# A DeltaNet, gating and Fourier step: the last base inverse is stepped beside the scan, inverse buffers get a pool of their own, inverses are stored in two halves

## The chip, the cores and the metric

The kernel runs on one core of a Trainium2 chip. The metric is the device time of one execution in microseconds; less is better. The core has TensorE for matrix products (PE, with its weight loads as PEld), VectorE (DVE), ScalarE (ACT), GpSimd (POOL), and SyncE (SP), which here only issues DMAs. Each engine works through its own list of instructions in order.

## The reference, cut to what matters

One layer of a model with three parallel token mixers, for 2048 sample tokens and 128 context tokens, width 1024:

```python
qkv, beta, dec, z_a, u_b, v_b, z_b, x_c, z_c, gates = jnp.split(xn @ w_in, points, -1)
o_a = rmsnorm(delta_bidir(l2norm(q), l2norm(k), v, g, beta, s0_f, s0_b)) * silu(z_a)
o_b = chunk_sgu(u_b, v_b, ...) * silu(z_b)
o_c = fourier_mix(x_c, grid) * silu(z_c)
pb = jnp.einsum('btnw,nwd->btnd', jnp.stack([o_a, o_b, o_c], 2), w_branch)
out = jnp.einsum('btnd,btnd->btd', sigmoid(gates), pb) @ w_out
# delta_bidir, per chunk and direction:
m = eye + b * (k k^T) * dec_strict            # unit lower triangular
u = solve(m, b * v - b * exp(gam) * k S)      # the reference solves for both parts first
o = exp(gam) * q S + ((q k^T) * dec_incl) u
S = exp(gam_last) * S + kd^T u                # S goes from chunk to chunk
```

The triangular solve and the walk of the state S over the chunks, forward and backward, are what the change is about.

## The kernel before, in words

Products are taken in pairs of 16-bit numbers (high and low part, three matmuls for one product; the helper with line L161 issues all of them). The sequence of the program is: normed x and z_a; q, k, v with their convolution; then the main line of big matrix products, which is the gating branch (to about 700 us), the Fourier branch (line numbers around L1243 to L1340, to about 1047 us), a first merge (the gating branch), a second (Fourier, to about 1720 us), a third (delta) and the output product.

The delta branch has no place of its own in this line. It is a generator, `delta()`, that a pace steps. After each unit of the main line the pace gets a number of units (`pace.tick`, `pace.part`), and it takes one step of the generator for each `quota` units: 1.6 during the preparation, 1.3 (`SCAN`) from the scan on. The order in which the program is written so mixes both; a scheduler that honours a few priorities then sets each engine's list from it. The same pace also moves the conversion of the weights along (`weight_step`).

The delta branch has these parts. 17 tiles of 128 tokens (tile 16 is the context) are prepared in five groups: (16), (0 to 3), (4 to 7), (8 to 11), (12 to 15). `prep` writes for each tile k, q, v, the products and the 32x32 diagonal blocks of the triangular matrices (nd) to DRAM. `base_inverse(g)` then inverts all diagonal blocks of a group at once on VectorE: 31 rounds of a product (L795, the tile names are XB and E) and a subtraction (L796), then a split into 16-bit halves on ACT and VectorE, and two stores (L805) to the DRAM array ei. The inverse of a group is stepped together with the preparation of the next group. The last group's has no next preparation: `for _ in base_inverse(4): yield 1` steps it alone, in 841 to 884 us. Then the memory pool of preparation and inverses (dqa) is closed, and one for the scan (dqb) is opened in its place.

`scan()` walks 34 iterations: forward over tiles 16, 0, 1, ... 15, then backward over 16, 15, ... 0. It has three chains. `level` builds the 128x128 inverses R from the 32x32 ones, reading ei (tiles ES, Q, T, R, N; cleared once in `zeroed`, L813, by POOL; evictions at L860 to L896). The chain of the state scales k (skn, L970), makes `v = sv - k S` (L908 after L907: the split into 16 bits, for v, u and S alike), `sv = R v` (L1001), u and the new S. `attend` makes the outputs o. The first S of a direction is scaled at L1024. A finished tile goes out through `finish`.

The Fourier branch evicts its products with copies and mirrored copies on VectorE (tiles X2, printed as X; L1285 to L1287), yT (L1304, L1305), and gates them on POOL (st, L1137), which stores them (br, L1139). At the merges' start the memory of the Fourier constants (cfp) is given back and the branch weights' pool (bwp) opened; `converting` makes from a staged weight (wst) its square sum with the scratch in blo (L209), the scaled high part (bhi, L222) and the low part (L223). Memory is shared in this way all over: a tile in a later pool waits for whatever lay at its address in the closed one.

Of the kernel before, what the change touches and what calls it, by code (L numbers as in the profile page):

```python
# [14 lines left out]
AF = mybir.ActivationFunctionType  # L15
ALU = mybir.AluOpType
# [4 lines left out]
P = 128  # L21
# [8 lines left out]
EPS = 1e-6  # L30
C_QKV, C_BD, C_ZA, C_U, C_V, C_ZB, C_XC, C_ZC, C_G = 0, 1536, 1552, 2064, 2576, 3088, 3600, 4112, 4624
QUOTA = 1.6
SCAN = 1.3
MT = 0.015
XB = 4
AD = (0, 2, 4, 6)
CQ = 545
FS = 4096.0
# [73 lines left out]
def hybrid_flow_kernel(ctx: ExitStack, tc: tile.TileContext, x_prompt, x_sample, state_delta, c, c_ctx, ln_g, w_ada,  # L112
# [3 lines left out]
    V, A, G, PE, SY = nc.vector, nc.scalar, nc.gpsimd, nc.tensor, nc.sync  # L116
    uid, rot = [0], [0]

    def nm(s):
        uid[0] += 1  # L120
        return f"{s}_{uid[0]}"

    def pool(stack, name, bufs, **kw):
        return stack.enter_context(tc.tile_pool(name=name, bufs=bufs, **kw))

    def sb(pl, shape, tag, dt=F32, bufs=None):
        kw = {} if bufs is None else {"bufs": bufs}
        return pl.tile(list(shape), dt, tag=tag, name=nm(tag), **kw)
# [17 lines left out]
    def dram(name, shape, dt=F32):  # L146
        return drp.tile(list(shape), dt, tag=name, name=name)
# [30 lines left out]
    def scales(ss, pl, tag, sb16=None):  # L178

        ps = bank(ps_x, [P, 1])  # L180
        mm(ps, ones16, widened(ss, pl, tag) if sb16 is None else sb16)
        t = sb(pl, [P, 4], tag)
        V.tensor_copy(t[:, 0:1], ps)
        h = t[:, 3:4].bitcast(I32)
        V.tensor_scalar(h, t[:, 0:1].bitcast(I32), 24, None, ALU.logical_shift_right)
        V.tensor_scalar(t[:, 1:2].bitcast(I32), h, -8388608.0, 204.0 * 8388608, ALU.mult, ALU.add)
        V.tensor_scalar(t[:, 2:3].bitcast(I32), h, 8388608.0, 50.0 * 8388608, ALU.mult, ALU.add)
        return t[:, 1:2], t[:, 2:3]
# [253 lines left out]
    for ti, (t0, tn) in enumerate(TBS):  # L442
        if t0 not in xts:
            load_x(t0, tn)
        g = 0 if t0 < NS else 1
# [10 lines left out]
        for k in range(KT):  # L456
# [3 lines left out]
            t = sb(p0p, [P, tn], "xm", bufs=3)  # L460
# [17 lines left out]
    def h3(ap):  # L478
        return ap.rearrange("p (h x) -> p h x", h=H)
# [7 lines left out]
    vqs = sb(dp, [P, 12], "vqs")  # L487
    decD = [dram(f"dec{t}", [P, 2, WB]) for t in range(NCH)]
    qkvD = dram("qkv", [12, P, LP - 2])
    dl = ExitStack()  # L490
    dq = pool(dl, "dqa", 1, side="right")
    cfs = ExitStack()
    CN = _CW - _CF
    cf = sb(pool(cfs, "cfp", 1), [P, 2, CN], "cf", F16)
# [16 lines left out]
    def decays():  # L511
# [71 lines left out]
        def rows_of(t):  # L583
            if t % 5 in (0, 1):
                row = sb(dq, [P, 2, WB], "dc", bufs=2)
            elif t % 5 == 2:
                row = sb(dq, [P, 1024], "E").rearrange("p (d x) -> p d x", d=2)
            else:
                if t % 5 == 3:
                    xb[0] = sb(dq, [P, 2048], "XB")  # L590
                row = xb[0][:, (t % 5 - 3) * 1024:(t % 5 - 2) * 1024].rearrange("p (d x) -> p d x", d=2)
            row = row.rearrange("p d (h i) -> p d h i", h=H)
            for d in range(2):
                SY.dma_start(row[:, d], gamR[d, t * H:(t + 1) * H, :].rearrange("h (o i) -> o h i", o=1).to_broadcast([P, H, P]))
            return row
# [5 lines left out]
        xb = [None]  # L601
# [20 lines left out]
    for ct in range(12):  # L622
        w = getw(1, 2 if ct < 6 else min(4, 15 - ct))
        for half in range(1):
# [12 lines left out]
            y = sb(a1p, [P, LP - 2], "cy")  # L637
# [26 lines left out]
    eD = [dram(f"ei{g}", [2, 32, len(ts), H * 512], F16) for g, ts in enumerate(GROUPS)]  # L664
# [109 lines left out]
    def base_inverse(g):  # L774
        nt = len(GROUPS[g])
        nb = 16 * nt
        XB = sb(dq, [P, 2048], "XB")
        X, tmp = XB[:, 0:1024], XB[:, 1024:2048]
        E = sb(dq, [P, 1024], "E")
        if nt < 4:  # L780
            V.memset(X, 0.0)
            V.memset(tmp, 0.0)
        b3 = lambda t_: t_.rearrange("p (j i) -> p j i", j=32)
        for d in range(2):
            SY.dma_start((X if d == 0 else tmp)[64 * d:64 * d + nb, :], ndD[g][d].rearrange("t h (b j) i -> (t h b) (j i)", b=4))
        for _ in range(8):
            yield 0
        V.tensor_copy(b3(X[64:P, :]), tmp[64:P, :].rearrange("p (i j) -> p j i", j=32))
        G.memset(E, 0.0)
        G.memset(E[:, 0:1024:33], 1.0)  # L790
        X3, E3 = b3(X), b3(E)
        for k in range(31, 0, -1):
            n_ = 32 - k
            t3 = tmp[:, 0:k * n_].rearrange("p (j i) -> p j i", j=k)
            V.tensor_tensor(t3, X3[:, 0:k, k:k + 1].to_broadcast([P, k, n_]), E3[:, k:k + 1, k:32].to_broadcast([P, k, n_]), ALU.mult)  # L795
            V.tensor_tensor(E3[:, 0:k, k:32], E3[:, 0:k, k:32], t3, ALU.subtract)  # L796
            if k % 2 == 0:
                yield 1
        both = XB.bitcast(F16).rearrange("p (j l w c) -> p j l w c", j=32, l=2, w=2)
        for w, src in ((0, E3), (1, E.rearrange("p (i j) -> p j i", j=32))):  # L800
            A.activation(both[:, :, 0, w, :], src, AF.Copy, scale=FS)
            V.scalar_tensor_tensor(both[:, :, 1, w, :], src, FS, both[:, :, 0, w, :], ALU.mult, ALU.subtract)
            yield 1
        for d in range(2):
            SY.dma_start(eD[g][d].rearrange("j t (y x) -> (t y) j x", x=128),  # L805
                         both[64 * d:64 * d + nb].rearrange("p j l w c -> p j (l w c)"))
            yield 1

    odd, wide, q_st, q_hi = [1], [], [], []

# [250 lines left out]
    def bounds():  # L1061

        nonlocal qs, us
        s0 = sb(dq, [P, 2, WB], "tok")
        for d in range(2):
            SY.dma_start(h3(s0[:, d]), state_delta[0, 0, d].rearrange("h k v -> k h v"))
        yield 1
        A.activation(sb(dq, [P, 1024], "E"), s0.rearrange("p d x -> p (d x)"), AF.Square, scale=math.sqrt(8.0), accum_out=vqs[:, 4:5])
# [14 lines left out]
    def delta():  # L1083
        nonlocal dq
        seq = [(g, ci, t) for g, ts in enumerate(GROUPS) for ci, t in enumerate(ts)]
        held = {1: rows(1, 16), 2: rows(2, 16), 0: rows(0, 16), "dc": decay_rows(16)}
        yield from bounds()
        base = iter(())
        for i_, (g, ci, t) in enumerate(seq):
            if ci == 0 and g:  # L1090
                for r_ in base:
                    if r_:
                        yield 1
                base = base_inverse(g - 1)
            for n_, _ in enumerate(prep(g, ci, t, seq[i_ + 1][2] if i_ < 16 else None, held)):
                yield 1
                if next(base, 0):
                    yield 1
        late(None, None)
        for r_ in base:  # L1100
            if r_:
                yield 1
        for _ in base_inverse(4):
            yield 1
        dl.close()
        dq = pool(dl, "dqb", 1, side="right")
        V.tensor_scalar(rq, rq, bnds[:, 2:3], None, ALU.mult)
        V.tensor_scalar(beta, beta, FS, None, ALU.mult)
        for d in range(2):
            V.tensor_tensor(eg[:, d], eg[:, d], rq, ALU.mult)  # L1110
        pace.quota, pace.fine = SCAN, True
        yield from scan()
        dl.close()
        dps.close()

    pace.start(delta(), QUOTA)


# [115 lines left out]
    for g in range(4):  # L1234
        xw, zw = getw(2, 2)
        for gh in range(1):
# [23 lines left out]
            for q in range(0, NCH, 4):  # L1260
                qn = min(4, NCH - q)
                ps = bank(ps_mm, [P, qn, P])
                for i in range(qn):
                    t = q + i
# [65 lines left out]
                gate_unit(2, g, ti, zw, yT[:, t0:t0 + tn], fronts[ti] if ti < 3 else silu_unit(ti, zw, zc), ti > 2)  # L1330
    fs.close()
    cfs.close()


    mD = dram("mrg", [KT, P, NTOK])
# [226 lines left out]
```

## Time and profile before

| what | value |
|---|---|
| median of 3 runs | 2200.02 us (2197.28 to 2202.29) |
| the profiled execution | 2200.34 us, its span 2198.2 us, mean granted clock 0.993 |
| scan | about 885 to 1686 us |
| last base inverse | about 841 to 884 us |

Times in the excerpts are microseconds from the start of the span unless marked ns. In a list of groups (`line engine op out<-in ... xN | busy, mean ns | idle before, releaser`) the number behind the second bar is the idle time of the engine just before these instructions, followed by what ended most of it. In a list of waits the three numbers are the sum, the number of waits and the longest. In the timeline a row has the start, the length, the engine, the line, operation and tile, and in brackets how long the engine stood still before it and what ended that. A table by stretches has the stretch, its length, then the busy time of PE, PEld, DVE, ACT, POOL (instructions in brackets), the mean granted clock of TensorE (1.00 is full speed), the busy share of the DMA engines, and GB/s.

### The profile page before, as it was taken

How to read it: one execution, taken by the hardware profiler on the slowest of the kernel's cores; microseconds unless marked ns; L12 is line 12 of the kernel's file. 1: busy time of each engine (PE TensorE's matmuls, PEld its weight loads, DVE VectorE, ACT ScalarE, POOL GpSimd, SP SyncE). 2: the span in 40 equal slices, each digit the busy share in tenths (PEclk: the TensorE clock that was granted, in tenths of full speed). 3: DMA queues.
4: the chain of work that ended last, by engine and by line, in shares of the span. 5: the costliest groups of instructions: out<-in, count | busy, mean ns of one | idle time of the engine just before them, and what ended most of it. 6: DMA issues, size and time to landing. Idle time of an engine off the chain costs nothing. (4 is left out here: it accounts for less than half of the span.)

```text
span 2198.2 us, 42667 instructions
## 1 busy us (share of the span) xinstructions
PE 2125.9 (97%) x16234; PEld 1213.1 (55%) x16234; DVE 1311.2 (60%) x3140; ACT 1014.4 (46%) x2345; POOL 707.5 (32%) x862
## 2 busy tenths in 40 slices
PE   7999999999999999899899999999999999999998
PEld 3565444455555587777555555555654444444443
DVE  5746745469979698466665555765674544223454
ACT  3644644345466474355544445655553422222332
POOL 1421433223333322432322223344532221222543
PEclk9999999999999999999999999999999999999999
DMA  8324733167777662444655556776664544324542
GB/s 280 141 87 149 260 117 110 61 203 231 241 229 239 198 192 83 126 130 137 203 172 162 164 164 185 240 212 209 200 198 151 168 125 133 118 78 123 174 148 103
DMA packets 304568, 365.09 MB, mean 166 GB/s; under 512 B 39426, under 2 KB 215787, under 8 KB 302315
## 3 DMA queue, kind: packets, MB, share of 16 engines
q1 hardware_dynamic: 289226, 302.19, 45.6%
q0 software_dynamic: 12688, 51.27, 6.4%
q10 hardware_dynamic: 2448, 8.91, 1.0%
q8 instruction: 127, 2.08, 0.4%
q14 instruction: 79, 0.64, 0.1%
HBM read 234.67 MB, written 127.62 MB: 165 GB/s over the span
## 5 line engine op out<-in xcount | busy, mean ns | idle before, releaser
L161 PE MATMUL b<-xh,whi 128*128 128x512 f16 (+1 forms) x1920 | 652.8, 349 | 0.4 <-DVE mrow L1391 0.4
L161 PE MATMUL b<-xl,whi 128*128 128x512 f16 (+1 forms) x1920 | 652.9, 348 | 0.0
L161 PE MATMUL b<-xh,wlo 128*128 128x512 f16 (+1 forms) x1920 | 651.9, 348 | 0.5 <-DVE wlo L223 0.5
L161 PEld LDWEIGHTS <-whi 128*128 128x128 f16 x3904 | 358.8, 98 | 330.0 <-issue 9.4
L161 PEld LDWEIGHTS <-wlo 128*128 128x128 f16 x1952 | 191.7, 98 | 180.8 <-issue 5.0
L161 PE MATMUL b<-big,bhi 128*128 128x512 f16 (+1 forms) x960 | 250.6, 347 | 2.4 <-ACT big L1355 1.9
L1395 POOL TENSOR_TENSOR mrow<-mrow,sg 128x512 f32<-128x512 f32 (+1 forms) x80 | 91.8, 1148 | 293.9 <-DVE sg L1394 225.7
L161 PE MATMUL b<-big,blo 128*128 128x512 f16 (+1 forms) x480 | 162.9, 347 | 0.0
L1385 ACT ACTIVATE sg<-b,winv 128x512 f32<-128x512 f32 (+1 forms) x120 | 74.1, 618 | 174.5 <-PE b L161 173.7
L644 POOL TENSOR_TENSOR cy<-cy,raw 128x545 f32<-128x545 f32 (+1 forms) x48 | 74.9, 1586 | 184.2 <-ACT raw L643 184.2
L161 PEld LDWEIGHTS <-xh 128*128 128x128 f16 x1496 | 117.0, 98 | 28.1
L1394 DVE SCALAR_TENSOR_TENSOR sg<-b,binv,sg 128x512 f32<-128x512 f32 (+1 forms) x80 | 53.4, 667 | 126.1 <-PE b L161 119.3
L161 PEld LDWEIGHTS <-bhi 128*128 128x128 f16 x960 | 86.5, 98 | 73.6 <-issue 2.1
L175 DVE CAST wscb<-wss 128x1 bf16<-128x1 f32 x93 | 14.3, 154 | 148.5 <-ACT wlo L209 67.3
L864 POOL COPY T<-ES 32x256 f16<-32x256 f16 x68 | 30.5, 449 | 202.3 <-DMA ES<-ei 167.1
L161 PE MATMUL b<-whi,xh 128*128 128x128 f16 x544 | 92.9, 219 | 0.0
L161 PE MATMUL b<-wlo,xh 128*128 128x128 f16 x544 | 92.9, 219 | 0.0
L161 PE MATMUL b<-whi,xl 128*128 128x128 f16 x544 | 92.9, 219 | 0.0
L161 PE MATMUL b<-wohi,mh 128*128 128x512 f16 x240 | 90.9, 379 | 1.4 <-ACT mh L1462 1.4
L161 PE MATMUL b<-wohi,ml 128*128 128x512 f16 x240 | 90.8, 379 | 0.3 <-DVE mscb L175 0.3
L161 PE MATMUL b<-wolo,mh 128*128 128x512 f16 x240 | 90.9, 379 | 0.0
L209 ACT ACTIVATE wlo<-wst 128x1024 f16<-128x1024 f32 x52 | 55.0, 1057 | 77.5 <-DMA wst<-in_w_in_dram 74.1
(456 smaller groups left out, 4285.4 us busy)
## 6 DMA issues: line engine op xcount, KB each, us to landing
wst<-in_w_in_dram SPq DMA_DIRECT2D x60, 512.0 KB, 4.9
qkv<-cy POOLq DMA_DIRECT2D x12, 1089.0 KB, 5.4
st<-br SPq DMA_DIRECT2D x48, 256.0 KB, 4.6
mrow<-mrg SPq DMA_DIRECT2D x18, 512.0 KB, 3.6
mrow<-mrg SPq DMA_DIRECT2D x16, 576.0 KB
mrg<-mrow POOLq DMA_DIRECT2D x16, 576.0 KB, 3.6
dc<-dec SPq DMA_DIRECT2D x17, 512.0 KB, 4.7
kq<-qkv SPq DMA_DIRECT2D x34, 256.0 KB, 4.6
```

The lines of the kernel that those rows point to most:

```text
L161: PE.matmul(out, l, r, start=start, stop=stop)
L175: V.tensor_copy(sb16, ss)
L209: A.activation(w.lo, st, AF.Square, accum_out=ss)
L644: G.tensor_tensor(y[:, c0:c1], y[:, c0:c1], raw[:, 1 + c0:1 + c1], ALU.mult)
L864: G.tensor_copy(T16[rows(a0, b), :, :, b], ES[0:32, :, 2 * a0 + b, :, wT])
L1385: A.activation(sg, ps, AF.Sigmoid, scale=gw.inv)
L1394: V.scalar_tensor_tensor(sg, ps, binv[:, 1:2], sg, ALU.mult, ALU.mult)
L1395: G.tensor_tensor(mr, mr, sg, ALU.add)
```

## The change

Three edits. First, E and XB, the buffers of the inverse (also used as scratch by two earlier steps), move from the pool dqa to one of their own, dqx, of 12288 bytes per partition, on the other side of the memory, open until the Fourier branch ends. Second, `base_inverse(4)` is no longer run to its end before the scan: the pool dqa is closed at once, and one step of the inverse is taken after each step of the scan; SCAN goes from 1.3 to 1.39. Third, each inverse is split and stored in two halves of 16 columns.

```diff
-SCAN = 1.3
+SCAN = 1.39
...
     dq = pool(dl, "dqa", 1, side="right")
+    dxs = ExitStack()
+    dx = pool(dxs, "dqx", 1)
...
-        XB = sb(dq, [P, 2048], "XB")
+        XB = sb(dx, [P, 2048], "XB")
         X, tmp = XB[:, 0:1024], XB[:, 1024:2048]
-        E = sb(dq, [P, 1024], "E")
+        E = sb(dx, [P, 1024], "E")
...
-        for w, src in ((0, E3), (1, E.rearrange("p (i j) -> p j i", j=32))):
-            A.activation(both[:, :, 0, w, :], src, AF.Copy, scale=FS)
-            V.scalar_tensor_tensor(both[:, :, 1, w, :], src, FS, both[:, :, 0, w, :], ALU.mult, ALU.subtract)
-            yield 1
-        for d in range(2):
-            SY.dma_start(eD[g][d].rearrange("j t (y x) -> (t y) j x", x=128),
-                         both[64 * d:64 * d + nb].rearrange("p j l w c -> p j (l w c)"))
-            yield 1
+        for js in (slice(0, 16), slice(16, 32)):
+            for w, src in ((0, E3), (1, E.rearrange("p (i j) -> p j i", j=32))):
+                A.activation(both[:, js, 0, w, :], src[:, js], AF.Copy, scale=FS)
+                V.scalar_tensor_tensor(both[:, js, 1, w, :], src[:, js], FS, both[:, js, 0, w, :], ALU.mult, ALU.subtract)
+                yield 1
+            for d in range(2):
+                SY.dma_start(eD[g][d, js].rearrange("j t (y x) -> (t y) j x", x=128),
+                             both[64 * d:64 * d + nb, js].rearrange("p j l w c -> p j (l w c)"))
...
-        for _ in base_inverse(4):
-            yield 1
+        base = base_inverse(4)
         dl.close()
         dq = pool(dl, "dqb", 1, side="right")
...
-        yield from scan()
+        for _ in scan():
+            yield 1
+            next(base, 0)
...
     fs.close()
     cfs.close()
+    dxs.close()
```

**In units of the pace** (counted in both programs; main-line units at which the delta branch reaches a place):

| place | before | after |
|---|---|---|
| last base inverse begins | 584.1 | 584.1 |
| scan begins (iteration 0) | 625.6 (655.1) | 584.1 (614.1) |
| iteration 17 (backward direction) | 920.2 | 897.8 |
| scan ends | 1189.0 | 1185.1 |
| first merge begins | 741.6, in iteration 5 | 741.6, in iteration 7 |
| second merge begins | 1002.7, in iteration 22 | 1002.7, in iteration 23 |
| last block of the second merge | 1231.2 | 1231.2 |

So an iteration takes (1189.0 - 655.1)/34 = 15.7 units before and (1185.1 - 614.1)/34 = 16.8 after.

**In memory.** Before, the scan's tiles S16, sk, o and sq_ lie on the places of XB and E. After, the first tiles of the scan (skn, sv, R, T, Q, N) lie on places of tiles loaded for the preparation (kq, qr), and S, kn16, v16 and sqk on those of n32 and n16. The Fourier constants lie 12288 bytes higher, and the weights' pool of the merges, which lay on their place before, now lies on the place of E.

**In the order of the engines.** First POOL, around the last gates of a Fourier group (st, stored as br) and the clearing of the scan's buffers (MEMSET). Before:

```order
L1139 DMA br_4087<-st_9463 128x512
L1137 TENSOR_TENSOR st_9497<-sg_9494,yT_8310 128x512
L1137 TENSOR_TENSOR st_9564<-sg_9561,yT_8310 128x128
L1139 DMA br_4087<-st_9497 128x512
L1139 DMA br_4087<-st_9564 128x128
L813 MEMSET R_1320_10487 128x1024
L813 MEMSET T_1321_10489 128x512
```

Now:

```order
L758 DMA nd_4098<-nd_9462 128x4x32 x2
L1140 TENSOR_TENSOR st_9476<-sg_9068,yT_8331 128x512
L1140 TENSOR_TENSOR st_9480<-sg_9138,yT_8331 128x512
L1140 TENSOR_TENSOR st_9484<-sg_9253,yT_8331 128x512
L815 MEMSET R_1272_9724 128x1024
L815 MEMSET T_1273_9726 128x512
```

The clearing stood behind a whole group's gates and stores, and now stands behind the first three gates of that group, right after the preparation's last store.

Second VectorE, around the scan's first row v (L908, now L910). Before:

```order
L1286 COPY X_1140_8304<-X_1140_8304 128x8x63
L1285 TENSOR_TENSOR X_1140_8304<-b_10337,X_1140_8304 128x4x63
L1304 TENSOR_TENSOR yT_9569<-b_10356,us_10381 128x8x32
L1305 TENSOR_TENSOR yT_9569<-b_10356,us_10381 128x8x32
L1287 TENSOR_SCALAR X_1140_8304<-X_1140_8304 128x8x63
L908 SCALAR_TENSOR_TENSOR v_1362_11064<-sv_10485,v_1362_11064 128x512
L1285 TENSOR_TENSOR X_1141_8305<-b_10395,X_1141_8305 128x4x65
L1286 COPY X_1141_8305<-X_1141_8305 128x8x63
L1024 TENSOR_SCALAR S_11058<-S_11058,usc_4243 128x512
```

Now:

```order
L797 TENSOR_TENSOR XB_9747<-XB_9747,E_9748 128x135
L798 TENSOR_TENSOR E_9748<-E_9748,XB_9747 128x27x5
L797 TENSOR_TENSOR XB_9747<-XB_9747,E_9748 128x156
L798 TENSOR_TENSOR E_9748<-E_9748,XB_9747 128x26x6
L910 SCALAR_TENSOR_TENSOR v_1323_10422<-sv_9722,v_1323_10422 128x512
L797 TENSOR_TENSOR XB_9747<-XB_9747,E_9748 128x175
L798 TENSOR_TENSOR E_9748<-E_9748,XB_9747 128x25x7
L1273 SCALAR_TENSOR_TENSOR xc_9695<-b_9598,xc_9695 128x512
L797 TENSOR_TENSOR XB_9747<-XB_9747,E_9748 128x192
L1026 TENSOR_SCALAR S_10416<-S_10416,usc_4246 128x512
```

Row v stood between two copies X of the Fourier branch; now it and the scaling of S stand among the rounds of the inverse (L797, L798), with a Fourier eviction (xc, L1273) between them.

Third ACT at the start of the first merge, between the first high part of a branch weight (bhi, L222) and the square sum of the second (blo, L209). Before:

```order
L222 ACTIVATE bhi_13405<-wst_11422,wsc_13413 128x512
L907 ACTIVATE u_13325<-sv_13071 128x512
L1385 ACTIVATE sg_13526<-b_13458,winv_12235 128x512
L894 ACTIVATE Q_10497<-b_13559 64x256
L860 ACTIVATE Q_1322_10491<-b_13626 32x256
L972 CAST kn_1600_13536<-skn_13499 128x512
L862 ACTIVATE Q_1322_10491<-b_13626 32x256
L209 ACTIVATE blo_14053,wss_14054<-wst_13741 128x512
L879 ACTIVATE R_1320_10487<-b_13650 64x4x64
L907 ACTIVATE S_1593_13482<-S_11058 128x512
```

Now:

```order
L222 ACTIVATE bhi_13821<-wst_11872,wsc_13829 128x512
L1141 ACTIVATE sg_13428,oss_481_4093<-st_13662 128x512
L909 ACTIVATE u_13714<-sv_13409 128x512
L209 ACTIVATE blo_14449,wss_14450<-wst_14137 128x512
L1389 ACTIVATE sg_13961<-b_13874,winv_12687 128x512
L896 ACTIVATE Q_9734<-b_13946 64x256
```

Six rows stood between bhi and blo, and two stand there now.

More of the change, by code (lines that the diff above doesn't have):

```diff
@@ L586, in rows_of @@
             elif t % 5 == 2:
-                row = sb(dq, [P, 1024], "E").rearrange("p (d x) -> p d x", d=2)
+                row = sb(dx, [P, 1024], "E").rearrange("p (d x) -> p d x", d=2)
             else:
                 if t % 5 == 3:
-                    xb[0] = sb(dq, [P, 2048], "XB")
+                    xb[0] = sb(dx, [P, 2048], "XB")
                 row = xb[0][:, (t % 5 - 3) * 1024:(t % 5 - 2) * 1024].rearrange("p (d x) -> p d x", d=2)
@@ L1067, in bounds @@
         yield 1
-        A.activation(sb(dq, [P, 1024], "E"), s0.rearrange("p d x -> p (d x)"), AF.Square, scale=math.sqrt(8.0), accum_out=vqs[:, 4:5])
+        A.activation(sb(dx, [P, 1024], "E"), s0.rearrange("p d x -> p (d x)"), AF.Square, scale=math.sqrt(8.0), accum_out=vqs[:, 4:5])
         V.tensor_reduce(bnds[:, 0:1], vqs[:, 0:4], AX.X, ALU.add)
```

## The prediction

> **What bounds the kernel now.** I read the page first, then the granted clock and busy time by stretches, then the waits of TensorE, then the timeline around the longest one.
>
> ```profile
> span 2198.2 us, 42667 instructions
> PE 2125.9 (97%) x16234; PEld 1213.1 (55%) x16234; DVE 1311.2 (60%) x3140; ACT 1014.4 (46%) x2345; POOL 707.5 (32%) x862
> ```
>
> TensorE is busy for 97% of the span, and the change adds and removes no matmul. So only what makes TensorE wait, or run at a lower clock, can be won or lost. By stretches (length, then busy time of PE, PEld, DVE, ACT, POOL, then clock):
>
> ```profile
> 480.00:880.00 400.00, 383.06 (x3154) 244.11 (x3152) 338.58 (x887) 224.00 (x665) 127.48 (x166) 0.99 0.66 203
> 880.00:905.00 25.00, 17.44 (x159) 11.02 (x157) 14.06 (x27) 8.91 (x20) 9.21 (x15) 0.86 0.66 155
> 905.00:1050.00 145.00, 143.17 (x2086) 118.06 (x2085) 85.94 (x219) 71.69 (x180) 47.39 (x72) 1.00 0.42 123
> ```
>
> The worst 25 us of the delta branch are 880 to 905: 7.6 us idle and a clock of 0.86. The waits between 876 and 905 us (who for whom: us in total, times, longest) say why:
>
> ```profile
> POOL R L813 <- DMA ei<-XB: 39.2, 1, 39.2
> ...
> PE b L161 <- DVE X L1286: 7.2, 1, 7.2
> ```
>
> and the timeline of the same stretch (start, length) shows the chain:
>
> ```profile
> 884.24 2.88 SPq L805 DMA_DIRECT2D ei<-XB  x2
> ...
> 892.73 0.95 POOL L813 MEMSET R<- 128x1024 f16 x1 [39.22 <-DMA ei<-XB]
> ...
> 898.15 0.69 DVE L908 SCALAR_TENSOR_TENSOR v<-sv,v 128x512 f16<-128x512 f32 x1 [6.49 <-DMA sn<-n]
> ...
> 900.28 0.48 PE L161 MATMUL b<-cf,X 128*128 128x128 f16 x3 [7.21 <-DVE X L1286]
> ```
>
> The scan's buffers take the place of the inverse's, so they wait until the last inverse is stored; the stores were issued from 884.24, and the first buffer was cleared at 892.73. The scan's row v stands in VectorE's order ahead of Fourier rows (second order excerpt above), waits for its load, and holds the copy X that TensorE wants.
>
> **What the change removes.** The base inverse now has memory of its own, and POOL's clearing of R follows the three products st (first excerpt). Nothing of the scan's start waits for the ei stores; those are wanted by the scan only at tiles 12 to 15. So the 7.21 us go. With them goes the slow clock behind the stall:
>
> ```profile
> 893.00:900.00 7.00, 0.07 (x2) 0.00 (x0) 1.81 (x3) 1.54 (x4) 6.97 (x9) 0.78 0.84 251
> 900.00:904.00 4.00, 3.72 (x12) 1.62 (x13) 2.61 (x7) 1.14 (x2) 1.10 (x3) 0.53 0.54 101
> ```
>
> 3.72 us of work at 0.53 cost 3.72 x 0.47 = 1.7 us. Together 8.9 us; the bounds are 0 (another row stalls as long) and 9.6 (all that is idle in 880 to 905, 7.6, and 2.0 of clock).
>
> **What it moves.** The first scan steps now lie beside the inverse, and VectorE has hardly room there:
>
> ```profile
> 845.00:892.00 47.00, 45.40 (x592) 35.96 (x590) 42.74 (x110) 19.18 (x39) 6.65 (x9) 1.00 0.30 73
> ```
>
> 4.3 us are free. In the order of the changed program I count the scan's rows that now stand ahead of the Fourier copies X for which TensorE stood still: one v, one S, one scaling of S, one sv, two Q of 32 partitions, three R or T of 32x128, one R and one Q of 64x256 (both at the R's price). Busy time, mean ns, idle before:
>
> ```profile
> L908 DVE SCALAR_TENSOR_TENSOR S<-S,S 128x512 f16<-128x512 f32 x32 | 28.9, 904 | 10.9 <-ACT S L907 10.4
> ...
> L908 DVE SCALAR_TENSOR_TENSOR v<-sv,v 128x512 f16<-128x512 f32 x34 | 27.1, 796 | 19.8 <-ACT v L907 13.0 <-DMA sn<-n 6.5
> ...
> L1001 DVE TENSOR_TENSOR sv<-b,beta 128x512 f32<-128x512 f32 x34 | 23.4, 688 | 15.4 <-PE b L161 14.7
> ...
> L880 DVE SCALAR_TENSOR_TENSOR R<-b,R 32x128 f16<-32x128 f32 x68 | 19.2, 283 | 21.1 <-ACT R L879 20.1
> ...
> L880 DVE SCALAR_TENSOR_TENSOR R<-b,R 64x256 f16<-64x256 f32 x34 | 14.1, 416 | 10.9 <-ACT R L879 10.2
> L861 DVE SCALAR_TENSOR_TENSOR Q<-b,Q 32x256 f16<-32x256 f32 x34 | 14.1, 416 | 17.5 <-ACT Q L860 16.7
> ...
> L1024 DVE TENSOR_SCALAR S<-S,usc 128x512 f32<-128x512 f32 x1 | 0.5, 486 | 0.1
> ```
>
> Work: 0.80 + 0.90 + 0.49 + 0.69 + 2 x 0.42 + 3 x 0.28 + 2 x 0.42 = 5.4 us. Their waits, by the mean idle time of each row (21.1/68 = 0.31 and so on; v without its 6.5): 0.39 + 0.34 + 0.45 + 2 x 0.51 + 3 x 0.31 + 2 x 0.32 = 3.8 us. VectorE would so come 5.4 + 3.8 - 4.3 = 4.9 us later to those X copies. TensorE also comes later, since its scan matmuls move ahead as well; twelve 128x128 and eight 128x32 of them take (timeline near 1053 us)
>
> ```profile
> 1053.29 0.83 PE L161 MATMUL b<-v,R 128*128 128x128 f16 x12
> ...
> 1055.18 0.35 PE L161 MATMUL b<-ES,N 128*128 128x32 f16 x8
> ```
>
> and one v R, two ES N and some 40 small ones of the levels (at about 0.04 each, as the second row has it) make 0.83 + 0.70 + 1.6 = 3.1 us. What comes back is 4.9 - 3.1 = 1.8, between 0 (no waits in so dense an order) and 4.9. I take 1.8.
>
> **The halves.** Every inverse now has four instructions instead of two on ACT and on VectorE, and four stores instead of two: 10 more on each engine and 10 more issues.
>
> ```profile
> L223 DVE SCALAR_TENSOR_TENSOR wlo<-wst,wsc,whi 128x1024 f16<-128x1024 f32 x52 | 71.2, 1375 | 29.6 <-ACT whi L222 29.3
> ...
> L223 DVE SCALAR_TENSOR_TENSOR blo<-wst,wsc,bhi 128x512 f16<-128x512 f32 x24 | 19.8, 824 | 1.8 <-ACT bhi L222 1.1
> ```
>
> and of the stores (KB each, us to landing)
>
> ```profile
> ei<-XB SPq DMA_DIRECT2D x8, 512.0 KB, 8.4
> ```
>
> Two halves cost 2 x 824 - 1375 = 273 ns more than one whole, 2.7 us of VectorE in five groups. It is 85% busy from 480 to 880, and TensorE idles 17 of those 400 us, so I let 0.5 us through; bounds 0 and 2.7. The stores shrink, and no wait is left for the last of them; the earlier groups' next load still waits for them, with a whole group of time in between, as before.
>
> **The wider pace.** A scan iteration takes 16.8 units of the pace instead of 15.7, the scan begins 41.5 units earlier and ends 3.9 earlier; the merge that needs it begins its last block 46 units behind its end, so no drain appears. About two of its 34 iterations leave the merges for the Fourier part. TensorE's waits between 1050 and 1700 us:
>
> ```profile
> PE b L161 <- ACT S L907: 5.3, 5, 2.5
> PE b L1055 <- ACT o L1051: 3.1, 4, 1.1
> ...
> PE b L161 <- DVE R L880: 1.8, 1, 1.8
> PE b L161 <- ACT Q L862: 1.8, 1, 1.8
> PE b L161 <- DVE S L908: 1.7, 4, 0.7
> ```
>
> They sum to 13.7 us for some 28 iterations, against 1.8 us of idle time from 905 to 1050 for six. Two iterations less are 1.0, and spacing wider by 7% perhaps 7% of the waits, 1.0; against that, the order is worked out anew. I take a gain of 1.5, between 0 and 3.
>
> **The first merge.** The branch weights' pool lies in the place of E instead of the Fourier constants, so the first blo moves forward by a Fourier group. The second still needs the first one's staging buffer (third excerpt):
>
> ```profile
> 1054.07 0.72 ACT L222 ACTIVATE bhi<-wst,wsc 128x512 f16<-128x512 f32 x1 [0.79 <-DVE wsc L186]
> ...
> 1059.85 0.63 ACT L209 ACTIVATE blo<-wst 128x512 f16<-128x512 f32 x1 [1.42 <-DMA wst<-in_w_branch_dram]
> ...
> 1060.74 0.62 ACT L907 ACTIVATE S<-S 128x512 f16<-128x512 f32 x1
> ...
> 1061.41 0.26 PE L161 MATMUL b<-S,sk 128*128 128x128 f16 x1 [2.52 <-ACT S L907]
> ```
>
> with this clock (0.57) behind it:
>
> ```profile
> 1060.00:1068.00 8.00, 6.42 (x44) 4.21 (x44) 6.05 (x18) 6.81 (x18) 1.62 (x4) 0.57 0.93 307
> ```
>
> The load takes 5.06 us from the end of bhi (1054.79) to 1059.85, and 5.06 - 1.42 = 3.6 of them were covered by the rows that stand between bhi and blo. Six rows stood there, two stand there now; two cover about a third, 1.2, so ACT can wait 2.4 us longer in front of S. Against that, the 2.52 us and 6.42 x 0.43 = 2.8 us of slow clock could go if S falls elsewhere. I take 0, between a gain of 5.3 and a loss of 4.8 (2.4 us of wait, as much again of clock).
>
> **The sum.** -8.9 + 1.8 + 0.5 - 1.5 + 0 = -8.1 us. The profiled execution took 2200.34 (span 2198.2 and 2.1 around it), 0.3 above the median of 2200.02; so 2192.2, or 2192 beside the median.
>
> **Rivals.** *The stall returns as a debt of VectorE* (chance 0.22). Its waits double (3.8 to 7.6), and POOL, idle in this stretch before, gets in its way. This trace has one such meeting, an inverse row of 135 elements during POOL's st:
>
> ```profile
> 849.47 1.41 POOL L1137 TENSOR_TENSOR st<-sg,yT 128x512 f32<-128x512 f32 x1 [0.83 <-DMA br<-st]
> ...
> 849.79 1.26 DVE L795 TENSOR_TENSOR XB<-XB,E 128x135 f32<-128x135 f32 x1
> ...
> 851.08 0.30 DVE L796 TENSOR_TENSOR E<-E,XB 128x135 f32<-128x135 f32 x1
> ```
>
> 1.0 us more than its partner. Two or three such meetings with the scan's products and copies cost 2.5 us. Then 1.8 + 3.8 + 2.5 = 8.1 come back instead of 1.8, and the time is 2198.5. The Trainium skill (SBUF — State Buffer, "Who interferes with whom") states that a VectorE instruction with two SBUF inputs contends with a POOL instruction that reads SBUF, one blocking the other for a whole instruction; the row at 849.79 agrees, and by the rule all 62 rows of this inverse are exposed. Against it: VectorE is that full in the inverses before too, beside a busy POOL.
>
> *The same blocking row, moved* (0.10, the slower side). Row v now stands a third into the inverse, and the S rows behind it. If their loads land late there, Fourier copies and inverse wait behind them with no slack left. With a wait w the sum is -8.1 + w: slower from w = 8.1 on, and about 2204 at w = 12, against 6.5 for this row before. Against it: the loads' buffers now lie where long-finished tiles were.
>
> *The first merge clears too* (0.13): its 5.3 us go, 2187.
>
> **How the numbers follow.** My forecast has 0.55, with its own range 2187 to 2197. The range 2184 to 2202 reaches into all rivals. Within 0.2% (4.4 us, about what this kernel's measurement can tell) means 2195.6 to 2204.4. Faster: 0.85 of the forecast, all of the first merge, a little of the debt: 0.63. Slower: the part of the moved row beyond 2204.4, and merges that take the new order badly by as much: 0.09. Same: the rest, 0.28.
>
> **What would show it.** Right: POOL's R is cleared near 847 us with no wait on ei; no TensorE wait over 3 us between 845 and 905; clock 1.0 there; the scan's first skn product before 860. The debt: VectorE over 95% busy from 845 to 895 and TensorE waiting for X. Wrong altogether: a wait of VectorE on v or S beside the inverse, or waits of TensorE on S, o, R and Q from 1050 to 1700 well above the 13.7 us of now.

## The result, and the profile after

| | median | runs | ratio to before, 95% interval |
|---|---|---|---|
| before | 2198.36 us | 15 | |
| changed | 2191.99 us | 15 | 0.9970 [0.9961, 0.9979] |

The change takes 6.4 us off, 0.3%. The forecast of 2192 was met. The trace shows that it was met by other ways than the ones forecast. The profiled execution after took 2189.4 us, 2.6 below its median, so the 10.9 us by which the two profiles differ overstate the gain. The page after:

```profile
span 2187.6 us, 42676 instructions
PE 2123.6 (97%) x16234; PEld 1214.9 (56%) x16234; DVE 1320.9 (60%) x3150; ACT 1015.0 (46%) x2355; POOL 701.6 (32%) x862
```

The same stretches as before the change (stretch, length, busy time of PE, PEld, DVE, ACT, POOL, then the clock), and the inverse's last part:

```profile
480.00:880.00 400.00, 381.51 (x3147) 243.43 (x3145) 342.57 (x893) 226.71 (x680) 143.21 (x189) 0.98 0.68 210
880.00:905.00 25.00, 24.63 (x288) 17.20 (x287) 17.93 (x47) 13.09 (x32) 2.80 (x7) 1.00 0.38 90
905.00:1050.00 145.00, 143.66 (x2140) 120.28 (x2138) 98.10 (x245) 73.81 (x189) 48.42 (x72) 1.00 0.46 139
845.00:892.00 47.00, 41.05 (x492) 31.20 (x490) 41.95 (x102) 21.02 (x47) 17.42 (x25) 0.93 0.45 129
```

The bad stretch of before, 880 to 905 us, is clean: 0.4 us idle and full clock. But the stretch ahead of it, 845 to 892, has lost much of what that one won: 5.9 us idle at a clock of 0.93, where it had 1.6 us and 1.00. The stall moved by 30 us. The timeline there shows how:

```profile
841.56 1.05 POOL L815 MEMSET R<- 128x1024 f16 x1 [0.76 <-DMA qk<-n]
...
845.66 0.69 DVE L910 SCALAR_TENSOR_TENSOR v<-sv,v 128x512 f16<-128x512 f32 x1 [0.25 <-ACT v L909]
...
849.01 1.05 POOL L972 TENSOR_TENSOR skn<-skn,ed 128x512 f32<-128x512 f32 x1
...
849.44 2.73 DVE L1026 TENSOR_SCALAR S<-S,usc 128x512 f32<-128x512 f32 x1 [1.59 <-DMA S<-in_state_delta_dram]
...
850.59 1.28 POOL L1140 TENSOR_TENSOR st<-sg,yT 128x512 f32<-128x512 f32 x1
...
852.20 0.63 ACT L909 ACTIVATE S<-S 128x512 f16<-128x512 f32 x1 [5.60 <-DVE S L1026]
852.73 0.58 ACT L1272 ACTIVATE xc<-b 128x512 f16<-128x512 f32 x1
...
855.82 0.27 PE L161 MATMUL b<-cf,xc 128*128 128x128 f16 x2 [2.08 <-DVE wsc L183]
...
867.64 0.42 DVE L863 SCALAR_TENSOR_TENSOR Q<-b,Q 32x256 f16<-32x256 f32 x1
...
868.09 0.37 ACT L864 ACTIVATE Q<-b 32x256 f16<-32x256 f32 x1 [4.25 <-DVE Q L863]
...
869.14 0.28 PE L161 MATMUL b<-cf,xc 128*128 128x128 f16 x2 [2.65 <-ACT xc L1272]
```

R is cleared at 841.6 without waiting for ei, and v is no longer late. But VectorE's scaling of S waited 1.59 us for its load and then took 2.73 us; the Fourier copy xc on ACT stood behind S, and the weight scale wsc and the next xc on VectorE behind the crowded inverse. Some 12 us later ACT stands 4.25 us for VectorE's row Q, which has its turn only among the inverse's rounds, and TensorE stands behind ACT's xc.

### The profile page after: what moved, and what is told of

It is laid out like the page before. It is cut to its first block, busy times and chain, and to the rows that moved or that the text cites. A ratio compares the mean times of both kernels' runs of the same rounds, so it can differ in the third digit from the quotient of the medians.

```text
span 2187.6 us, 42676 instructions
## 1 busy us (share of the span) xinstructions
PE 2123.6 (97%) x16234; PEld 1214.9 (56%) x16234; DVE 1320.9 (60%) x3150; ACT 1015.0 (46%) x2355; POOL 701.6 (32%) x862
## 3 DMA queue, kind: packets, MB, share of 16 engines
q8 instruction: 127, 2.08, 0.4%
## 4 chain that ended last, share of the span: by engine, by line
PE 50%; DMA 4%; DVE 4%; ACT 1%; issue 1%; POOL 0%; SPq 0%; DVEq 0%; POOLq 0%; ACTq 0%
PE b L161 50%; DMA st<-br 1%; DMA ES<-ei 1%; DMA mrg<-mrow 1%; DMA wst<-in_w_in_dram 0%; DVE XB L797 0%; DVE E L798 0%; DVE big L1360 0%; DMA mrow<-mrg 0%; DMA S<-in_state_delta_dram 0%; DMA wst<-in_w_branch_dram 0%; PE b L1057 0%; ACT big L1359 0%; DMA sq__2210_18514<-qT 0%; DMA qk<-n 0%
## 5 line engine op out<-in xcount | busy, mean ns | idle before, releaser
L161 PEld LDWEIGHTS <-whi 128*128 128x128 f16 x3904 | 358.1, 98 | 329.2 <-issue 10.2
L646 POOL TENSOR_TENSOR cy<-cy,raw 128x545 f32<-128x545 f32 (+1 forms) x48 | 66.4, 1408 | 185.7 <-ACT raw L645 185.7
L209 ACT ACTIVATE wlo<-wst 128x1024 f16<-128x1024 f32 x52 | 54.9, 1056 | 77.4 <-DMA wst<-in_w_in_dram 75.5
```

Of the source, the lines that this page charges most:

```text
L161: PE.matmul(out, l, r, start=start, stop=stop)
L209: A.activation(w.lo, st, AF.Square, accum_out=ss)
L646: G.tensor_tensor(y[:, c0:c1], y[:, c0:c1], raw[:, 1 + c0:1 + c1], ALU.mult)
```

## A measure by stages

A single profile varies: the same program's executions lie some 10 us apart (before: 2194.0 to 2204.2). To compare stages I took, from each trace, the time from each matmul's start to the next one's, less the lower quartile of that time over all matmuls of the same form. What is left over is TensorE's lost time, waits and slow clock together. (Where the expectations below speak of idle TensorE time in a stage, they mostly mean this lost time.) Each kernel's time less its sum is 2110.2 to 2111.7 us in all rows below, so these sums carry the differences. In us, by stages of the span:

| kernel | to 475 | 475 to 845 | 845 to 925 | 925 to 1050 | 1050 to 1100 | 1100 to 1425 | 1425 to 1725 | rest | sum | its time |
|---|---|---|---|---|---|---|---|---|---|---|
| before | 18.6 | 24.1 | 11.4 | 2.5 | 11.9 | 10.2 | 8.2 | 2.7 | 89.7 | 2200.3 |
| before, second profile | 17.8 | 21.5 | 12.0 | 3.4 | 13.5 | 6.5 | 7.1 | 2.7 | 84.6 | 2195.5 |
| changed | 17.0 | 19.9 | 9.9 | 1.5 | 14.0 | 4.9 | 9.4 | 2.5 | 79.2 | 2189.4 |
| own pool alone | 17.0 | 24.5 | 7.0 | 3.8 | 14.6 | 6.8 | 6.5 | 3.4 | 83.6 | 2195.3 |
| own pool alone, second | 17.4 | 22.3 | 7.0 | 3.5 | 14.5 | 9.7 | 7.5 | 3.9 | 85.8 | 2196.9 |
| pool and joint stepping | 17.3 | 22.4 | 16.9 | 0.3 | 8.8 | 9.6 | 7.2 | 4.0 | 86.7 | 2197.1 |
| change without pace | 18.2 | 22.2 | 16.2 | 0.3 | 10.8 | 8.8 | 7.8 | 2.9 | 87.2 | 2197.5 |
| without pace, stores on POOL | 16.1 | 22.6 | 10.6 | 1.2 | 9.2 | 11.5 | 6.2 | 2.6 | 80.2 | 2191.9 |

Two profiles of one program differ by up to 3.7 us in a stage (1100 to 1425), 2.6 in 475 to 845, and by 0.6 or less in 845 to 925. Differences of the size of these are not read as effects below. That scale rests on two pairs of profiles only.

The stage 845 to 925 can be split at 885 us, just ahead of where the inverse's stores begin when they stand beside the scan. What is lost ahead of 885 lies beside the crowded VectorE; what is lost behind 885 is within reach of the stores. (In the kernel before, the 7.2 us stall ahead of X lies there.)

| kernel | 845 to 885 | 885 to 925 |
|---|---|---|
| before, and second profile | 1.6, 1.4 | 9.8, 10.6 |
| own pool alone, both profiles | 6.0, 6.0 | 1.0, 1.0 |
| pool and joint stepping | 7.9 | 9.0 |
| change without pace | 8.8 | 7.4 |
| without pace, stores on POOL | 6.7 | 4.0 |
| changed | 9.4 | 0.5 |

## Experiments: the change built up edit by edit

**The own pool alone.**

```diff
# of the whole change only: E and XB in dqx.
# The last inverse is run to its end first, SCAN = 1.3, whole stores.
```

> Only the first edit: E and XB in a pool of their own; the last inverse still alone ahead of the scan, SCAN 1.3, whole stores. If the stall of 7.2 us and its slow clock come from the shared memory, they go without any debt of VectorE, and the time is about 2198.4 - 8.9 = 2189.5. If the stall belongs to the scan's first rows wherever they stand (loads of v and S that arrive late, as in the changed kernel, where 841 to 905 us lost only 2 us of TensorE's idle time), about 2196.

Measured: 2198.01 us, ratio 1.0001 [0.9989, 1.0012]: no gain that shows (the interval allows 2.4 us), and later than either figure expected. Yet the stage of the stall is better. So I took a second profile of each:

> The kernel before, unchanged, for a second profile. If the 7.2 us stall ahead of X is the program's and no accident, it is there again within 1 us; the waits that differ by more than 1 us between the two profiles are those that a single profile cannot be trusted on.

> The kernel with only the separate pool, unchanged, for a second profile. Its first profile took 2195.3, 2.7 below its median, and showed 7.0 us of idle TensorE time in 850 to 925 instead of 11.4. If the stall's removal is real but given back elsewhere, 850 to 925 stays near 7 and one later stage (925 to 1100 or the merges) shows more than in the kernel before; if it is not real, 850 to 925 is back near 11.

Waits of TensorE (845 to 925 us) in the second profile of before, and that stretch:

```profile
PE b L161 <- DVE X L1286: 7.4, 1, 7.4
...
845.00:925.00 80.00, 71.18 (x952) 57.15 (x949) 51.41 (x131) 30.18 (x65) 23.83 (x34) 0.94 0.36 98
```

The same with the pool alone, second profile:

```profile
PE b L161 <- DVE xc L1272: 2.1, 3, 0.9
PE b L161 <- DVE wsc L183: 1.2, 1, 1.2
...
845.00:925.00 80.00, 75.90 (x1047) 63.28 (x1045) 55.33 (x139) 31.89 (x69) 27.73 (x40) 0.98 0.36 109
```

Both look as in their first profiles: the 7 us stall is the program's, and a pool of its own removes it, for 4.7 us in this stage (11.7 to 7.0 by the table), not 8.9. The waits on xc and wsc take the rest. That the whole time did not follow is not fully settled: in both profiles 1050 to 1100 shows 1 to 3 us more and the stages from 1725 on 1 more, and the merges between vary too much to tell. The single times of the two second profiles, 2196.9 with the pool and 2195.5 without, tell nothing by themselves.

**Joint stepping with the pool.**

```diff
# own pool, and:
-        for _ in base_inverse(4):
-            yield 1
+        base = base_inverse(4)
...
-        yield from scan()
+        for _ in scan():
+            yield 1
+            next(base, 0)
```

> Own pool and joint stepping of the last inverse, but SCAN 1.3 and whole stores. By the prediction's sum 2198.4 - 8.9 + 1.8 = 2191.3. If the joint stepping only moves the stall (the trace of the change has 9.4 us of idle TensorE time in 850 to 925 where there were 11.4), about 2196.

Measured: 2199.84 us, ratio 1.0010 [0.9998, 1.0021]. It is no gain, again later than either figure expected, and if anything a loss of 2 us on the pool alone, which the intervals do not separate from nothing. The stage 845 to 925 goes from 7.0 to 16.9 us lost; 925 to 1050 and 1050 to 1100 get 3 and 6 of it back. Of the 9.9 us that are new, 8.0 lie behind 885 us, and most of these have one cause, in this timeline (VectorE's last split, then the queue of SP, then TensorE):

```profile
886.74 0.35 PE L161 MATMUL b<-ES,N 128*128 128x32 f16 x8
...
888.15 1.94 DVE L804 SCALAR_TENSOR_TENSOR XB<-E,XB 128x1024 f16<-128x1024 f32 x1 [0.67 <-ACT XB L803]
...
890.12 2.89 SPq L807 DMA_DIRECT2D ei<-XB  x2
893.10 6.25 SPq L853 DMA_DIRECT2D N<-n  x6
...
893.51 0.28 PE L161 MATMUL b<-ES,Q 128*128 128x64 f16 x4
...
899.46 1.28 SPq L849 DMA_DIRECT2D ES<-ei  x3
...
902.83 0.45 PE L161 MATMUL b<-ES,N 128*128 128x32 f16 x8 [6.00 <-DMA ES<-ei]
```

The inverse's stores are now in the middle of the scan's loads, and SP issues its DMAs in the order of its list. The matmul at 886.74 is the last reader of N, but N's loads for the next tile stand behind the stores, and the stores wait for VectorE's split (to 890.1). ES comes behind N, at 899.5, some 6 us after its own last reader started (893.51), and TensorE stands 6.0 us for it.

**The halves added.**

```diff
# the whole change, but
-SCAN = 1.39
+SCAN = 1.3
```

> The whole change but SCAN 1.3. By the prediction the wider pace is worth 1.5 us, so 2193.5. If the merges' gain in the trace (5.3 us less idle TensorE time in 1100 to 1425) is the pace's work, about 2196.

Measured: 2197.40 us, ratio 1.0000 [0.9987, 1.0014]. This is before's time. Everything but the pace gives no gain that shows. The same place:

```profile
887.52 4.22 SPq L808 DMA_DIRECT2D ei<-XB  x4
...
891.84 4.72 SPq L853 DMA_DIRECT2D N<-n  x6
896.67 1.29 SPq L849 DMA_DIRECT2D ES<-ei  x3
...
901.07 0.47 PE L161 MATMUL b<-ES,N 128*128 128x32 f16 x8 [3.30 <-DMA ES<-ei]
```

The first store goes 2.6 us earlier than a whole one, and TensorE waits 3.3 instead of 6.0 us for ES, which now goes out 1.7 us after its last reader started (894.94).

**What the pace adds.** From here to the whole change only SCAN differs, and the ratio goes from 1.0000 to 0.9970: 6.6 us, with some 3.6 either way. In the changed kernel:

```profile
885.21 4.22 SPq L808 DMA_DIRECT2D ei<-XB  x4
...
887.97 0.35 PE L161 MATMUL b<-ES,N 128*128 128x32 f16 x8
...
890.93 3.89 SPq L853 DMA_DIRECT2D N<-n  x6
895.41 1.23 SPq L849 DMA_DIRECT2D ES<-ei  x3
```

N still goes out 3 us behind its last reader. ES no longer waits for the queue: its last reader starts at 895.07, and the load goes out 0.34 us later. And TensorE has more of the main line in front of the next tile's level: it comes to ES at 906.50, without a wait. The stage loses 9.9 us instead of 16.2, all of it won behind 885 us (0.5 instead of 7.4). From 1050 to 1725 the change loses 28.3 us by the table and the kernel without the pace 27.4, so no gain of the pace shows in the merges.

## Experiments: what the pace does

> The kernel before with SCAN 1.39 and nothing else. The whole change with SCAN 1.3 was no faster than before, so the pace is worth some 5 us in company with the joint stepping. If it is worth that by itself, in the merges: about 2193. If it only takes the scan's second tile out of the way of late loads while the inverse is stored beside the scan, there is nothing to take here: about 2198, within 2 us of before.

```diff
# the kernel before, with
-SCAN = 1.3
+SCAN = 1.39
```

Measured: 2198.99 us, ratio 1.0004 [0.9991, 1.0017]. The pace by itself gives nothing; TensorE's stall ahead of X is there (7.8 us). It works only with the joint stepping. There it does so without the halves too: pool and joint stepping have the ratio 1.0010, and 0.9987 with the pace added (the run without halves, below), 5.1 us with some 3.8 either way.

If so, taking the stores out of SP's queue should do the same without the pace:

```diff
# the whole change, SCAN = 1.3, and
-                SY.dma_start(eD[g][d, js]...
+                (SY if g < 4 else G).dma_start(eD[g][d, js]...
```

> The whole change with SCAN 1.3, and the last group's four stores issued by POOL instead of SP. With SCAN 1.3 the loads of the scan's next tile (N, then ES) stood on SP behind these stores, which wait for VectorE's split, and TensorE waited 3.3 us for ES, with a slower clock behind it. If that is what the wider pace cures, about 2197.5 - 3.3 - 2 = 2192. If the pace works in another way, 2197, or later if POOL's own rows behind the stores come late.

Measured: 2193.59 us, ratio 0.9980 [0.9969, 0.9990], against 1.0000 with the stores on SP: 4.4 us, with some 3.8 either way.

```profile
885.29 0.36 PE L161 MATMUL b<-ES,N 128*128 128x32 f16 x8
885.65 3.54 SPq L853 DMA_DIRECT2D N<-n  x6
886.29 3.35 POOL L808 DMA_DIRECT2D ei<-XB  x4 [10.18 <-DVE XB L805]
...
893.10 0.28 PE L161 MATMUL b<-ES,Q 128*128 128x64 f16 x4
893.44 1.23 SPq L849 DMA_DIRECT2D ES<-ei  x3
...
897.41 0.43 PE L161 MATMUL b<-ES,N 128*128 128x32 f16 x8 [1.46 <-DMA ES<-ei]
```

N is issued 0.36 us after its last reader starts, where it was 3.58 us behind the stores; ES 0.34 us, where it was 1.73. The wait falls from 3.30 to 1.46 us, and the stage loses 10.6 instead of 16.2 us. Of these 5.6 us, 3.4 lie behind 885 us, where the queue can be the reason; the other 2.1 lie ahead of the stores and are something else. POOL stood 10.2 us for the split, at no cost that shows. So the queue on SP is a part of what the wider pace gets around. It is not the whole: the 1.46 us that remain are a wait for a load that already went out 0.34 us after the last reader's start, and the pace, which puts other work in front of it, leaves 0.5 us behind 885 where the stores on POOL leave 4.0.

> The changed kernel (SCAN 1.39) with the last group's four stores issued by POOL. TensorE waits for no ES there, so nothing is to be gained by this theory: 2192, within 2 us. If SP's queue also delays other loads that matter, 2189.

Measured, with the pace and the stores on POOL: 2193.03 us, ratio 0.9972 [0.9961, 0.9983]. That is the changed kernel's ratio: the two remedies do not add up, as expected.

## Experiments: the halves

```diff
# no_halves: the whole change with the old, whole splits and stores
# halves_only: the kernel before with the new splits and stores
```

> The whole change but whole splits and stores. By the prediction the halves cost 0.5 us, so 2191.5. If the 3.6 us less of idle time in 475 to 850 are the halves' work, about 2195.5.

Measured: 2195.11 us, ratio 0.9987 [0.9974, 1.0000]; the change with halves has 0.9970. So the halves are worth 3.7 us here, with some 3.5 either way. They are not won at the stall: without halves the stage 845 to 925 loses 9.8 us, with them 9.9, and TensorE waits for no ES in either. The two profiles differ by 2.7 us in 475 to 845 and 1.8 in 1050 to 1100, about as much as two profiles of one program.

> The kernel before with the splits and stores in halves and nothing else. The prediction put 0.5 us on them (2198.6). The change without them measured 3 us more than with them, at the edge of what can be told; if that gain is the halves' own, in the preparation from 475 to 845 us, about 2195.

Measured: 2196.54 us, ratio 1.0000 [0.9986, 1.0014]. Alone they are worth nothing and cost nothing that can be seen in the time. The stage of the stall does gain from them: it loses 8.3 us (11.4 and 12.0 before), and TensorE's longest wait there is 4.7 us instead of 7.2. In this one profile the stores go out from 878.5 instead of 884.2 us, and R is cleared at 886.6 instead of 892.7, after a wait for a row X and not for ei. As with the own pool, the whole time does not follow. The preparation's stage, 475 to 845, has no clear sign either way (21.5 us lost, as in the second profile of before). What they are worth beside the joint stepping stands at the edge of the intervals; where it would come from was not shown.

## Experiments: what is left of the stall

```diff
# the change, with S loaded ahead of the scan's prologue, and scaled on ACT:
-                    V.tensor_scalar(S2, S2, us, FS, ALU.mult, ALU.mult)
+        A.activation(S0, S0, AF.Copy, scale=bnds[:, 4:5])   # bnds[:, 4:5] holds us * FS; direction 1 likewise
```

> The changed kernel with the first S loaded ahead of the scan's prologue and scaled on ACT instead of VectorE. In the change VectorE's scaling of S waited 1.6 us for its load and then took 2.7 us beside two POOL rows, where it takes 0.5 alone; ACT stood 5.6 us for it, and TensorE 2.7 us behind ACT's copy xc. If this row is what remains of the stall, 2.7 us and about 1 us of slow clock go: 2188 to 2189. If VectorE's debt to the inverse is what holds the copies, another row takes its place: 2192.

Measured: 2189.65 us in 6 runs, ratio 0.9959 [0.9944, 0.9973]. It is the fastest kernel of the study, 2.4 us under the change by ratio, but the two intervals overlap. S and TensorE's two waits there:

```profile
847.38 0.72 ACT L967 ACTIVATE S<-S,bnds 128x512 f32<-128x512 f32 x1 [0.94 <-DMA S<-in_state_delta_dram]
...
855.25 0.27 PE L161 MATMUL b<-cf,xc 128*128 128x128 f16 x2 [1.81 <-DVE wsc L183]
```

S is ready 4 us earlier (848.1 against 852.2), and neither ACT's xc nor TensorE stands for it. But TensorE's wait on wsc only falls from 2.08 to 1.81 us. The rows of POOL and VectorE ahead of wsc show where the time went:

```profile
848.79 1.59 POOL L976 TENSOR_TENSOR skn<-skn,ed 128x512 f32<-128x512 f32 x1
...
849.40 1.83 DVE L797 TENSOR_TENSOR XB<-XB,E 128x207 f32<-128x207 f32 x1
...
850.93 1.44 POOL L1146 TENSOR_TENSOR st<-sg,yT 128x512 f32<-128x512 f32 x1
...
851.27 1.33 DVE L798 TENSOR_TENSOR E<-E,XB 128x207 f32<-128x207 f32 x1
```

With S out of the way, this round of the inverse lies beside the same two rows of POOL, and takes 1.83 and 1.33 us where it took 0.38 and 0.36 in the change: 2.4 us more, about as much as S had lost there. So, as far as this one trace shows, the loss goes to whichever row of VectorE lies beside these products, and is not S's own; the stage loses 9.0 us (9.9 with the change).

```diff
# besides, in the levels, ACT's second copy Q ahead of VectorE's difference Q
-        V.scalar_tensor_tensor(Qf[64:96, ...], src, 1.0 / FS, Qf[0:32, ...], ALU.mult, ALU.subtract)
         A.activation(Qf[32:64, ...], src, AF.Copy, scale=1.0 / FS)
+        V.scalar_tensor_tensor(Qf[64:96, ...], src, 1.0 / FS, Qf[0:32, ...], ALU.mult, ALU.subtract)
```

> The changed kernel with S loaded early and scaled on ACT, and in the levels the second copy Q of ACT (32 partitions) ahead of VectorE's difference Q instead of behind it. In the change ACT stood 4.3 us for that row of VectorE, which stood behind seven rows of the inverse, and TensorE 2.7 us for the copy xc behind it. If that wait goes, about 2189.7 - 2.5 = 2187. If xc waits for another row of VectorE instead: 2189.7.

Measured: 2198.45 us, ratio 1.0010 [0.9996, 1.0023]: 8.8 us slower than without this swap by the medians, 11 by the ratios. What ACT waited for ahead of its rows Q, in the kernel without the swap:

```profile
  PE b L161: 25.4, 21
  DVE Q L863: 18.8, 20
```

and with it:

```profile
  PE b L161: 30.2, 23
```

The swap did what it should: 18.8 us of ACT's waits, 20 of them, are gone, and the xc wait of 2.3 us has become one of 1.5 on VectorE. The time went the other way, since the stretch of the merges changed: TensorE's idle time there rose from 18.8 to 22.5 us (1050 to 1725 us; first row without, second with the swap):

```profile
1050.00:1725.00 675.00, 656.19 (x5497) 380.29 (x5495) 396.76 (x1034) 340.18 (x860) 228.04 (x301) 0.99 0.61 186
```

```profile
1050.00:1725.00 675.00, 652.55 (x5470) 378.24 (x5468) 390.17 (x1030) 338.71 (x858) 225.47 (x300) 0.99 0.60 183
```

One wait in it, of TensorE on ACT's copy big, went from 0.9 to 3.4 us. By the measure of the stages, which counts slow clock too, the merges (1050 to 1725) lose 34.2 us with the swap and 28.3 without. These 5.9 us are as much as the two profiled executions differ (2194.3 and 2188.3), but two profiles of one program differ by up to 3.8 there. Why the merges lose more was not found. It also sets a scale for this kernel: two instructions changing places can move the whole by as much as the change under study.

## Why the prediction was right, step by step

**The sum was right, and most of its terms were not, so it is in good part luck that the total came out.** In time, 2198.0 before; own pool 0 (within 2.5); joint stepping about +2; halves about -2; pace -6.6. The prediction had -8.9 for the memory, +1.8 for the move, +0.5 for the halves, -1.5 for the pace: a gain of 8.1, where 6.4 was measured. The figure 2192 was helped further by its starting point, the 2200.02 of 3 runs; from the 2198.36 of all 15 the same sum gives 2190.3, 1.7 us from what was measured.

- *What the change removes, -8.9.* The mechanism is as told: the clearing of R and the row v wait no more, and 880 to 905 us is clean. The size is off: with the pool alone the stage gained 4.7 us, twice, since other rows of VectorE (xc, wsc) stall TensorE in place of X. And no gain that shows arrived at the end of the kernel. The lower bound of this term, 0, is what was measured, within 2.5 us (the upper bound counts 2.0 us of clock, which no row shows as such; 17.44 us at 0.86 are 2.4); why the stage's gain is not in the total stays open.
- *What it moves, +1.8 (0 to 4.9).* At SCAN 1.39 the stage loses 2.9 us more than with the pool alone (9.9 against 7.0), inside the bounds. At SCAN 1.3 it loses 9.2 to 9.9 more. That is as much as the rival "debt" was priced at (8.1), but only 1.9 to 2.8 of it lie ahead of 885 us, beside the inverse; 6.4 to 8.0 lie behind it, where the stores are.
- *The rival "debt"* came in part, beside the forecast. Ahead of 885 us the changed kernel loses 3.4 us more than the own pool alone. The meetings with POOL are there: the scaling of S took 2.2 us longer than before, a round beside kn 1.0 us longer than its partner (rows in the last section), 3.2 together against the 2.5 of the rival. Its signs are not: VectorE is 90% busy from 845 to 895 (over 95% was named), and TensorE waits for wsc and xc, for X only 0.4 us.
- *The step that failed* is the sentence on the halves' stores, "no wait is left for the last of them". True of the scan's buffers, it missed SP's order: the stores, which wait for VectorE, came to stand ahead of the loads of N and ES, which had nothing to do with them. TensorE's wait for ES was 6.0 us with whole stores and 3.3 with halves, of which 1.46 remained with the stores on POOL. In the changed kernel itself it costs nothing that shows, since the wider pace has TensorE come to ES later.
- *The wider pace, -1.5 in the merges.* The sign came true for another reason. Alone it gave 1.0004, and beside the joint stepping 6.6 us, where by the table the stage 845 to 925 won 6.3. In the merges TensorE's waits (1050 to 1700, all rows) went from 18.5 to 17.9 us, not by the 1 us and 1 us forecast; the 13.7 of the prediction were the sum of the five rows that it showed.
- *The first merge, 0 (-5.3 to +4.8).* The lost time there is 14.0 us against 11.9 and 13.5. The wait of ACT in front of blo was forecast to grow by 2.4 us from 1.42; it grew by 2.05, and what stood behind it was not S but sg, Q and kn:

```profile
1057.16 0.63 ACT L209 ACTIVATE blo<-wst 128x512 f16<-128x512 f32 x1 [3.47 <-DMA wst<-in_w_branch_dram]
...
1058.48 0.38 ACT L896 ACTIVATE Q<-b 64x256 f16<-64x256 f32 x1
...
1059.71 0.51 PE L161 MATMUL b<-R,Q 128*128 128x64 f16 x12 [2.82 <-DVE Q L897]
```

- *The moved row.* The rival named v; it was S, with a wait w of 1.6 us and 2.2 us of longer work. Moving S away won little, since the round of the inverse that took its place lost as much. Row v did stand a third into the inverse, with a wait of only 0.25 us.
- *The signs to look for.* R cleared near 847 (841.6) and the first skn product before 860 (849.0) came true, and no wait of TensorE in 845 to 905 passes 3 us (the longest is 2.65). Full clock there did not: 0.93 over 845 to 892.

What cannot be told: where all of the 6.4 us lie. By the table the change against the mean of the two profiles of before has 1.8 us less in 845 to 925 and 1.5 less in 925 to 1050, 1.3 more in 1050 to 1100 and 1.8 more in 1425 to 1725; the larger gains, 2.9 in 475 to 845 and 3.5 in 1100 to 1425, are about as large as the difference of two profiles of one program (2.6 and 3.7).

## What to carry to other kernels

When work that ends in a store is moved beside other work, look at the queue that issues the store: a store that waits for a busy engine holds every load behind it on that queue, and the consumer that pays is one that the store has nothing to do with. Build such a change up edit by edit, because parts that give nothing alone (the pace) or cost something alone (the joint stepping) may only work as a pair. And in a program with an order as tight as this one, removing a wait by exchanging two instructions may cost more in a distant stage than it brings, so only the time of the whole tells.

## What the hardware did that was not expected

VectorE's scaling of S, 128x512 in 32 bits with one input in SBUF, took 2.73 us where it took 0.49 before. Its start lay in POOL's product skn and its end 0.3 us behind POOL's product st (849.01 to 850.06 and 850.59 to 851.87, rows above). A round of the inverse beside POOL's kn took 1.38 us and its partner 0.42:

```profile
859.02 1.90 POOL L975 TENSOR_TENSOR kn<-skn,kn 128x512 f16<-128x512 f32 x1 [1.03 <-ACT kn L974]
```

```profile
859.83 1.38 DVE L797 TENSOR_TENSOR XB<-XB,E 128x252 f32<-128x252 f32 x1
861.24 0.42 DVE L798 TENSOR_TENSOR E<-E,XB 128x252 f32<-128x252 f32 x1
```

The Trainium skill (SBUF — State Buffer, "Who interferes with whom") names both kinds: a VectorE instruction with two SBUF inputs contends with a POOL instruction that reads SBUF, and tensor_scalar can enter a mode that takes both port pairs, in which whoever comes second is blocked for the whole instruction. The round at 859.83 agrees with it: it starts inside POOL's kn and ends 0.3 us behind it. The S row outlasted POOL's skn and then st as well, which is more than one whole instruction; that it was in such a mode is not shown by the trace. Also not expected: the six loads of N took 6.25 us of SP's time behind the whole stores, 3.89 behind those of the changed kernel, and 3.54 with the stores on POOL, which were issued in the same microseconds. What sets these times was not found.
